# One late store of a cross-covariance attention kernel: transfers of 119 and 9 partitions in place of 92, 4, 32 and a half

## The chip, the cores and the metric

The kernel runs on one core of a Trainium2 chip. Its time is in device microseconds, the median of several runs; lower is better. The profile is of one execution, and its span runs from the core's first instruction to its last.

The core has a matrix engine (TensorE, here PE, with its weight loads as PEld), VectorE (DVE), ScalarE (ACT), GpSimd (POOL) and SyncE (SP). SP computes nothing here: it issues nearly all of the transfers between device memory and on-chip memory. The transfers themselves are carried out by sixteen DMA engines, which work through what has been issued.

## The reference

Q, K and V have 8 batches, 12 heads, 512 rows and 64 columns, in float32. For each of the 96 batch-heads, Q and K are normalised along the rows, their product over the rows gives a 64 x 64 matrix, its rows go through a softmax, and V is multiplied with the result:

```python
Q_norm = Q / (np.linalg.norm(Q, axis=-2, keepdims=True) + 1e-10)
K_norm = K / (np.linalg.norm(K, axis=-2, keepdims=True) + 1e-10)
attn = np.einsum('bhnd,bhne->bhde', Q_norm, K_norm)
attn = np.exp(attn - np.max(attn, axis=-1, keepdims=True))
attn = attn / (np.sum(attn, axis=-1, keepdims=True) + 1e-10)
return np.einsum('bhnd,bhde->bhne', V, attn).astype(np.float32)
```

The three inputs are read once (37.75 MB) and the output is written once (12.58 MB).

## The kernel before

**Tiling.** Four heads make a unit, of which there are 24, and two units make a step `s`, of which there are 12 (`S`). Q and K of a unit are loaded with 4 KB or 8 KB per partition, cast to bf16 by DVE (`cast_qk`, L208), and PE forms the Gram matrices of Q and K together (`grams`, L220), from which both the norms and the product come. DVE, ACT and POOL take them through the scaling and the softmax. V of two steps is loaded together (`load_v`, L189), cast, transposed on PE (`vtrans`, L294), and multiplied with the softmax result (`outs`, L309). The product is copied into a tile `so` by `ocopy` (L320, ACT or DVE).

**Stores.** A step has two output tiles, `so[s, 0]` and `so[s, 1]`, each of 128 partitions with two rows of 512 float32: the middle index `r` picks one row of 2 KB, and both are 512 KB together. `store(s, i)` (L198) writes tile `i` of step `s`. There are 24 stores; I write them (s, i). Each is one transfer of 128 partitions with both rows, L206, apart from one: `FEW = (S - 3, 1)` (L122), which is store (9,1). Four stores come behind it: (10,0), (10,1), (11,0) and (11,1), which is the last transfer of the kernel. A row of 2 KB on one partition is one DMA packet.

**Order.** The class `Order` (L22) plans the whole program ahead of time from estimated costs. Every piece of work has the engines it may run on, what it needs, what it stands behind, and a rank, and the plan picks the piece that can begin first, ranks deciding among those that are close. The program is then written in that order, so each engine's stream is fixed when the kernel is built. For the plan a store is one piece, of fixed cost `X`, however many transfers `store` makes of it.

**Issue on SP.** SP works its list off in order. A store waits for its two copies. It also waits for a completion semaphore: the transfers from SP and ACT take eight of them in turn, so a transfer can be issued only when the one eight places earlier has landed in full, that is when every DMA engine that had a share of it has reported. A DMA engine adds one to the semaphore when its share has landed. At the end of the program SP waits for the transfers still on their way (L493), and then the engines meet in a few barriers.

**Instructions.** PE has 4320 matmuls and weight loads. Instructions are also brought in through the DMA engines, which the profile shows as queues of their own: q8 with packets of 16 KB, q14 with packets of 8 KB.

Of the kernel before, what the change touches and what calls it, by code (L numbers as in the profile page):

```python
# [102 lines left out]
def kernel(  # L103
# [7 lines left out]
    nc = tc.nc  # L111
# [50 lines left out]
    qk32, v32, vb, qkb, gram, scr, kq, n2, r8, kqs, rq, lg, ex, ab, vps, vt, po, so = ({} for _ in range(18))  # L162
# [35 lines left out]
    def store(s, i):  # L198
        o = Of[s // 2, s % 2, i].rearrange("p r (j d) -> p r j d", d=D)
        if (s, i) == FEW:  # L200

            for a, b in ((0, 92), (92, 96), (96, 128)):
                nc.sync.dma_start(out=o[a:b, 0], in_=so[s, i][a:b, 0])
            nc.sync.dma_start(out=o[:, 1], in_=so[s, i][:, 1])
            return
        nc.sync.dma_start(out=o, in_=so[s, i])  # L206

# [139 lines left out]
    for i in range(NB["ab"]):  # L347
        a = const.tile([128, HU, 2 * D], BF16, name=f"ab{i}")
# [42 lines left out]
    for u in range(U):  # L391
        s, r = divmod(u, 2)
# [48 lines left out]
    for s in range(S):  # L441
        for x in range(4):
            i, k = divmod(x, 2)
            n = 4 * s + x - 2
            wait = [("oc", n // 4, n % 4)] if n >= 0 else []
            order = [("ou", s, x - 1) if x else back("ou", s, 1, 3)]
            piece(("ou", s, x), {"PE": 0.5}, [("vc", s // 2, *t) for t in turns(s // 2) if t[0] // 2 == k] + [("nm", s)] + wait, order, R["ou"] + 0.01 * s, outs, s, x)
            n = 2 * s + i - NB["so"]
            free = [("st", n // 2, n % 2)] if k == 0 and n >= 0 else []
            order = [("oc", s, x - 1) if x else back("oc", s, 1, 3)]  # L450
            piece(("oc", s, x), {"ACT": 0.6, "DVE": (0.68, BIAS["oc"])} if s >= BOTH else {"ACT": 0.6}, [("ou", s, x)] + free, order, R["oc"] + 0.01 * s, ocopy, s, x)
        for i in range(2):
            order = [("st", s, 0) if i else back("st", s, 1, 1)]
            piece(("st", s, i), {"DMA": X}, [("oc", s, 2 * i), ("oc", s, 2 * i + 1)], order, v_at(2 * s + i) + ST_LAG, store, s, i)
# [43 lines left out]
```

## Time and profile before

| what | value |
|---|---|
| median of 3 runs | 129.41 us (129.15 to 129.7) |
| span of the profiled execution | 127.43 us; the profile gives no other time for it |
| DMA traffic | 50.66 MB, 14958 packets, 398 GB/s in the mean |
| share of 16 DMA engines, kernel's transfers (q1 and q10) | 98.0% |
| PE busy | 77.0 us (60%) |
| DVE busy | 92.9 us (73%) |
| ACT busy | 72.3 us (57%) |
| POOL busy | 37.0 us (29%) |
| last copy into an output tile ends | 116.6 us |
| first transfer of store (9,1) issued | 111.44 us |
| store (11,1) issued | 120.75 us |

How to read the profile: the span is cut into 40 equal slices, and each digit is the busy share of an engine in a slice in tenths, 9 being 90% or more. The DMA row is the mean over the sixteen DMA engines, and the GB/s row what they moved. The queue table gives packets, megabytes and the share of the sixteen engines' time for each queue. A view can be limited to a window of the span, and then the 40 slices divide the window. The table of waits gives who waited for whom: microseconds in total, times, and the longest. Beside these the trace holds the time of every landing, one for each DMA engine's share of a transfer, and the start, length, size and queue of every DMA packet, but not the number of the DMA engine that moved it.

### The profile page before, as it was taken

To read this page: it belongs to the slowest core of one execution; us is meant where nothing else is said; L and a number is where in the kernel's file an instruction comes from. 1 tells how busy PE (TensorE), PEld (TensorE's weight loads), DVE (VectorE), ACT (ScalarE), POOL (GpSimd) and SP (SyncE) were. 2 spreads that over 40 slices of the span, in tenths; PEclk is the share of its full clock that TensorE was granted. 3 is DMA by queue.
4 is the path that set the end of the run, shared out by engine and by line. 5 is a ranking of instruction groups with operands and counts; after the bars stand their busy time and mean duration, and the time that the engine had idled before them with its cause. 6 is when DMAs were issued, how large, how long until landed. Compare 5 with 4: busy or idle time off the path is not lost.

```text
span 127.4 us, 4949 instructions
## 1 busy us (share of the span) xinstructions
PE 77.0 (60%) x2160; PEld 62.7 (49%) x2160; DVE 92.9 (73%) x142; ACT 72.3 (57%) x220; POOL 37.0 (29%) x39
## 2 busy tenths in 40 slices
PE   0065393994837679859475986777597729753000
PEld 0054372783636568647354674666386517541000
DVE  3344749949899899999974989998999499950000
ACT  4000441559877077886691897583848919996000
POOL 4006307300916903033077011303733160300000
PEclk9999999999985555999996799869959995999755
DMA  4999999999999999999999999999999999999991
GB/s 113 413 438 408 428 411 418 417 433 408 435 418 414 411 417 424 402 415 427 423 414 414 415 428 417 415 424 425 401 420 419 401 402 410 395 408 408 375 377 60
DMA packets 14958, 50.66 MB, mean 398 GB/s; under 512 B 1112, under 2 KB 1112, under 8 KB 13400
## 3 DMA queue, kind: packets, MB, share of 16 engines
q1 hardware_dynamic: 14648, 49.29, 95.9%
q10 hardware_dynamic: 288, 1.05, 2.1%
q8 instruction: 17, 0.28, 0.8%
q14 instruction: 5, 0.04, 0.1%
HBM read 37.75 MB, written 12.58 MB: 395 GB/s over the span
## 4 chain that ended last, share of the span: by engine, by line
DVE 36%; PE 21%; DMA 19%; issue 8%; ACT 5%; SPq 1%; DVEq 0%; ACTq 0%
DVE qkb L212 15%; DMA qk<-in_K_dram 14%; PE gram L232 12%; DVE scr L239 7%; DMA qk<-in_Q_dram 5%; DVE vt L168 4%; PE vps L301 4%; DVE ab L290 4%; PE po L318 3%; ACT so L166 3%; DVE n L251 2%; ACT ex L281 2%; DVE vb L168 2%; PE lg L275 1%; SPq L185 1%
## 5 line engine op out<-in xcount | busy, mean ns | idle before, releaser
L232 PE MATMUL gram<-qkb 32*128 32x128 bf16 x1536 | 36.7, 259 | 24.8 <-issue 8.5
L232 PEld LDWEIGHTS <-qkb 32*128 32x128 bf16 x1536 | 30.8, 116 | 29.7 <-issue 11.1
L212 DVE CAST qkb<-qk 128x1024 bf16<-128x1024 f32 x48 | 37.7, 810 | 9.6 <-DMA qk<-in_Q_dram 8.0
L170 POOL TENSOR_SCALAR vb<-v 128x1024 bf16<-128x1024 f32 x18 | 21.7, 1215 | 43.9 <-DMA v<-in_V_dram 39.0
L166 ACT COPY vt<-vps 128x1024 bf16<-128x1024 bf16 (+1 forms) x18 | 17.8, 986 | 18.8 <-PE vps L301 18.7
L166 ACT COPY so<-po 128x512 f32<-128x512 f32 x45 | 24.9, 593 | 6.1 <-PE po L318 5.8
L318 PE MATMUL po<-ab,vt 128*64 128x128 bf16 x384 | 19.1, 237 | 6.2 <-issue 2.6
L262 POOL TENSOR_TENSOR kqs<-kq,r 64x512 f32<-64x512 f32 x12 | 14.0, 1169 | 29.1 <-ACT r L258 16.2
L301 PE MATMUL vps<-identb,vb 128*128 128x128 bf16 x192 | 18.5, 253 | 4.8 <-POOL vb L170 3.5
L239 DVE SCALAR_TENSOR_TENSOR scr<-gram,eye 64x512 f32<-64x512 f32 x24 | 16.5, 687 | 4.9 <-PE gram L232 4.7
L318 PEld LDWEIGHTS <-vt 128*64 128x64 bf16 x384 | 13.4, 117 | 10.4 <-issue 5.7
L301 PEld LDWEIGHTS <-vb 128*128 128x128 bf16 x192 | 14.0, 113 | 7.9 <-POOL vb L170 4.2
L281 ACT ACTIVATE ex<-lg,rq 128x64 f32<-128x64 f32 x48 | 14.5, 322 | 2.7 <-PE lg L275 2.6
L166 ACT COPY kq<-gram 64x512 f32<-64x512 f32 x12 | 7.0, 582 | 13.2 <-DVE scr L239 12.9
L290 DVE TENSOR_TENSOR ab<-ex,rinv 64x256 bf16<-64x256 f32 x24 | 12.8, 534 | 0.6
L281 ACT ACTIVATION_READ_ACCUMULATOR ex<-lg,rq 128x1 f32 x48 | 10.2, 213 | 0.0
L168 DVE CAST vb<-v 128x1024 bf16<-128x1024 f32 x6 | 7.4, 1241 | 1.8 <-DMA v<-in_V_dram 1.7
L275 PE MATMUL lg<-eye,kqs 64*128 64x64 f32 x48 | 6.4, 259 | 3.2 <-issue 1.6
L251 DVE TENSOR_REDUCE n<-scr 128x8 f32<-128x512 f32 x12 | 8.1, 679 | 0.1
L168 DVE COPY vt<-vps 128x1024 bf16<-128x1024 bf16 (+1 forms) x8 | 8.0, 1022 | 0.2
L275 PEld LDWEIGHTS lg<-eye,kqs 64*128 64x128 f32 x48 | 4.5, 156 | 5.0 <-issue 2.5
L287 DVE RECIPROCAL rinv<-esum 128x4 f32<-128x4 f32 x12 | 2.0, 170 | 2.5 <-ACT ex L281 2.4
(17 smaller groups left out, 16.0 us busy)
## 6 DMA issues: line engine op xcount, KB each, us to landing
v<-in_V_dram SPq DMA_DIRECT2D x12, 1024.0 KB, 17.4
out_dram<-so SPq DMA_DIRECT2D x23, 512.0 KB, 11.2
qk<-in_Q_dram SPq DMA_DIRECT2D x8, 1024.0 KB, 16.8
qk<-in_K_dram SPq DMA_DIRECT2D x8, 1024.0 KB, 18.8
qk<-in_Q_dram SPq DMA_DIRECT2D x8, 512.0 KB, 11.9
qk<-in_K_dram SPq DMA_DIRECT2D x6, 512.0 KB, 12.6
qk<-in_K_dram ACTq DMA_DIRECT2D x2, 512.0 KB, 7.3
out_dram<-so SPq DMA_DIRECT2D x1, 256.0 KB, 7.2
```

The lines of the kernel that those rows point to most:

```text
L166: nc.scalar.copy(o, i)
L168: nc.vector.tensor_copy(o, i)
L170: nc.gpsimd.tensor_scalar(out=o, in0=i, scalar1=1.0, scalar2=0.0, op0=ALU.mult, op1=ALU.add)
L212: nc.vector.tensor_copy(qkb[u][:, :, x * D:(x + 1) * D], qk32[s][:, x, r])
L232: nc.tensor.matmul(gram[s][:, h, r, 0], x, x, start=(t == 0), stop=(t == (T if u < WIDE else J) - 1))
L239: nc.vector.scalar_tensor_tensor(out=scr[s][half], in0=gram[s][half, :, :, 0, half].rearrange("p h r d -> p (h r) d"), scalar=1e-20, in1=e ...
L262: (nc.vector if eng == "DVE" else nc.gpsimd).tensor_tensor(out=kqs[s][HI], in0=kq[s][HI], in1=r8[s][HI, :, None].to_broadcast([D, 2 * HU, ...
L275: nc.tensor.transpose(l[:, h, :], kqs[s][HI, 2 * h:2 * h + 2].rearrange("p r d -> p (r d)"), eye2[HI])
L281: nc.scalar.activation(e[:, h, :], lg[s][:, h, :], AF.Exp, scale=rq[s][:, h:h + 1], accum_out=z[:, h:h + 1])
L290: nc.vector.tensor_tensor(out=a[half, :, half], in0=e[half], in1=ri[half, :, None].to_broadcast([D, HU, D]), op=ALU.mult,)
L301: nc.tensor.transpose(ps[:, c, n, :], vb[w][:, J * c + j].rearrange("p r d -> p (r d)"), identb)
L318: nc.tensor.matmul(po[s, x][e * D:(e + 1) * D, j].rearrange("p r d -> p (r d)"), v, ab[s][:, h, :])
```

## The change

Store (9,1) is split differently. Before, row 0 of the tile leaves in three transfers, of partitions 0 to 91, 92 to 95 and 96 to 127, and row 1 in one transfer of all 128 partitions. After, both rows leave together, in one transfer of partitions 0 to 118 and one of partitions 119 to 127. SP issues two transfers fewer. The bytes are the same, the plan is the same, and all other stores and loads are as they were.

```diff
         o = Of[s // 2, s % 2, i].rearrange("p r (j d) -> p r j d", d=D)
         if (s, i) == FEW:
 
-            for a, b in ((0, 92), (92, 96), (96, 128)):
-                nc.sync.dma_start(out=o[a:b, 0], in_=so[s, i][a:b, 0])
-            nc.sync.dma_start(out=o[:, 1], in_=so[s, i][:, 1])
+            for a, b in ((0, 119), (119, 128)):
+                nc.sync.dma_start(out=o[a:b], in_=so[s, i][a:b])
             return
         nc.sync.dma_start(out=o, in_=so[s, i])
```

## The prediction

> **What bounds the kernel now.** I read the slices of the span first. DMA is at nine tenths or more in every slice between the first and the last, while no compute engine stays busy, so bytes on the sixteen DMA engines set the time. The queue table adds that almost all of it is the kernel's own traffic (q1), with 17 packets of instructions (q8) beside it.
>
> ```profile
> DMA  4999999999999999999999999999999999999991
> DMA packets 14958, 50.66 MB, mean 398 GB/s; under 512 B 1112, under 2 KB 1112, under 8 KB 13400
> q1 hardware_dynamic: 14648, 49.29, 95.9%
> q8 instruction: 17, 0.28, 0.8%
> ```
>
> So what a change in a late store can move is how the sixteen engines finish against each other. The window from 124.7 us to the end, in 40 slices of 0.07 us, shows it:
>
> ```profile
> DMA  3513110000000000000000000000000000000000
> GB/s 117 205 59 117 59 59 29 29 29 29 0 29 29 29 29 29 29 29 0 29 29 0 0 0 0 0 0 0 0 0 0 0 0 0 0 0 0 0 0 0
> ```
>
> 29 GB/s is one 2 KB packet per slice: from 125.1 to 126.2 us a single engine works and fifteen have finished. The same in the window from 125.5 us, where 9 packets are left:
>
> ```profile
> DMA packets 9, 0.02 MB, mean 9 GB/s; under 512 B 1, under 2 KB 1, under 8 KB 9
> ```
>
> Why one engine is last is in the trace's record of landings, sixteen per store (one per engine). In us:
>
> ```
> store (9,0):  116.39 116.46 116.54 116.86 116.87 117.23 117.63 118.48
>               119.16 119.17 119.27 119.28 119.29 119.39 119.42 120.69
> store (11,1): 123.55 123.57 123.68 124.34 124.37 124.75 125.11 125.12
>               125.13 125.21 125.22 125.24 125.34 125.36 125.50 126.53
> ```
>
> Ahead of the changed store, (9,1), there are seven early engines, one at 118.48, seven within 0.26 us, and one late. The 17 instruction packets (16 KB each) explain the groups: they last 967, 967, 948, 879, 881, 935, 929, 931 ns, then 960, 964, 951, 881, 879, 935, 931, 921, then 960. The same eight durations come round again, so eight engines take turns; each time an engine falls about 1.4 us back ((119.3-116.46)/2). Seven of the eight have had two; the seventeenth, at 117.65 us, gave one its third. That engine is the last at 126.53, and 0.9 us of barriers follow to the end of the span. Stores of 32 KB per engine keep this order, since each engine takes 1.27 us for one.
>
> **Profile against times.** The span is 127.43 us, the median of the runs 129.41 (129.15 to 129.7). The page gives no other time for the profiled execution, so I take 1.98 us outside the span as fixed. 0.5% of the time, 0.65 us, is about what a measurement of this kernel tells from no change.
>
> **The change, part by part.** How a transfer is spread is read from two rows. There are 71 issues; 71 x 16 is 1136 completions, the page counts 1112 small packets, 24 fewer. The parts of 92 and of 4 partitions complete on 4 engines each, which is 2 x 12. So 92 goes to 4, 4 to 4, 32 and 128 to 16: the largest number up to 16 that divides the partitions. By this 119 goes to 7 engines (17 partitions each) and 9 to 9. The Trainium skill ("DMA: Bandwidth & Descriptors", Why a DMA increments its semaphore by 16) has this rule, and adds that the lowest-numbered engines are used; it also tells of direct copies of the other descriptor path that put 8 partitions on an engine regardless, which is the third rival below.
>
> Packets of 2 KB per engine for store (9,1): before, the first four get 23+1+2+8 = 34, the other twelve 2+8 = 10. After, the first seven 17 x 2 = 34 and 2 more from the second transfer, 36; engines eight and nine get 2; the last seven get 0. Both sum to 256.
>
> Price of a packet: the late engine goes from 120.69 to 121.47 in store (9,1), 0.78 us for 10 packets and two completions; 32 KB stores take 1.27/16 = 0.080 us. The four engines of the 92 part landed it at 118.31, 118.70, 119.08, 119.47: 1.83 to 1.85 us after four of the early landings (116.46, 116.87, 117.23, 117.63), 23 packets at 0.080. So packing many onto few engines cost no more per packet there. The other end is a stretch of nine packets in a row between 98.5 and 99.7 us on one engine, 98 to 182 ns each, 0.13 in the mean: 34 packets would take 1.7 us longer. I take 0.080, the nearest row in place and kind, and keep 0.13 for the range.
>
> - Late engine: it loses 10 packets (if among the last seven) or 8 (if eighth or ninth). 126.53 - 0.78 = 125.75, or 126.53 - 0.61 = 125.92.
> - First four: two packets more, two completions fewer: 125.50 + 0.16 - 0.02 = 125.64 for the latest.
> - Fifth to seventh: if they are the remaining early ones (116.39, 116.54, 116.86), the latest gets 116.86 + 36 x 0.080 + 0.02 = 119.75, then four stores as the late engine did them (126.53 - 121.47 = 5.06): 124.81.
> - The engine at 118.48 with two packets: 118.48 + 0.17 + 5.06 = 123.7. The pack: 119.42 + 5.06 = 124.5.
>
> The end is 125.75 to 125.92. It can't go below 125.64 without the first four, so the gain is at most 0.89.
>
> Issues and waits. SP issues two transfers fewer (0.32 to 0.37 us each). Eight completion semaphores are used in turn, so the four stores behind wait for landings two places earlier: (11,0) and (11,1) for 115.55 and 116.85 in place of 119.65 and 120.69. They leave at about 115.6 and 116.9, not 119.72 and 120.75; (10,0) and (10,1) then wait for their copies, at about 113.1 and 114.6. Worth nothing at the end: only the three earliest engines ran dry (they did (10,1) by 120.25 and (11,0) at 122.28 to 122.40), and after the change they have work till 119.75. No other queue issues anything here, and the other engines' programs are untouched.
>
> ```profile
> SPq L493 <- DMA out_dram<-so: 5.3, 4, 1.6
> SPq L206 <- DMA out_dram<-so: 4.7, 4, 2.4
> SPq L204 <- DMA out_dram<-so: 0.9, 1, 0.9
> SPq L203 <- DMA out_dram<-so: 0.9, 1, 0.9
> ```
>
> These are SP's waits from 112 us on; I expect L206's to nearly vanish and those at the end (L493) to grow.
>
> Sum: gain 0.61 to 0.78, middle 0.70; 129.41 - 0.70 = 128.7. Own range of this case with the spread of the runs: 128.4 to 129.0.
>
> One rule of the skill bears on the late engine. The row: an instruction packet takes 879 to 967 ns and the engine under it lands 1.4 us late. "Runtime: NRT & Kernel Launch", Instruction fetch mechanics, says PE refills 256 instructions, 16 KB, at a time (4320 PE instructions make 17: agreed) and that the cost is "mostly hidden". By that the sixteen would be level and this change only a loss, the fifth to seventh ending 26 x 0.080 = 2.1 us behind the rest; the measured lag decides against it, and it gets no chance of its own.
>
> **Rivals.**
>
> *The seven take in an engine that is not early (slower).* The trace doesn't number engines. It shows that the four of the 92 part are early; that the next three are too is inferred from eight engines that fetch and eight that don't, and a block of eight. If one of the pack is among them: 119.42 + 2.90 + 5.06 = 127.38, 0.85 later, 130.3; with the late engine itself, 131.5. It decides from a landing of store (9,0) later than 126.53 - 5.06 - 2.90 = 118.57.
>
> *They take in the engine at 118.48.* 118.48 + 2.90 + 5.06 = 126.44: 0.09 gained, 129.3, no change. It is one of the eight that never fetch, so it may as well be fifth to seventh as eighth.
>
> *The split does nothing: 119 goes out eight partitions to an engine.* Then every engine gets 16, the late one 6 more: +0.48, 129.9. Against: 92 went to four engines. This stays inside 0.5%.
>
> *Few engines are slow.* At 0.13 us a packet the latest of the first four gets 125.64 + 1.7 = 127.3, 0.8 later, 130.2. Against: the 92 part's 0.080.
>
> **How the numbers follow.** Main case 0.62; an engine that is not early 0.20; the one at 118.48 0.10; no split 0.03; slow packets 0.05. In the main case 0.61 and 0.78 lie on both sides of 0.65; the late engine is first in the turn of eight, which may be the block's first (8 packets) or another (10), so I put somewhat over half of it, 0.38, above 0.5% and 0.24 within. Same is 0.24 + 0.10 + 0.03 = 0.37, slower 0.20 + 0.05 = 0.25. The range holds the main case with the spread, 118.48 and one of the pack: 128.4 to 130.3.
>
> **What would show it.** Right: the first transfer completes on 7 engines, small packets 69 x 16 - 9 - 7 = 1088; the one-engine stretch at the end shorter, the last landing near 125.8; SP's last four issues by 117 us. Wrong: several engines, about three, alone at the end and the last landing after 126.5 (first rival), or 1097 small packets, 7 missing and not 16 (no split). Should the late engine in other executions have had only two fetches, 125.50 against 125.64 would be left and nothing gained.

## The result and the profile after

The changed kernel takes 130.22 us (median of 7, 130.01 to 131.33) against 129.41 us (median of 7, 129.05 to 129.7): a ratio of 1.0079, with a 95% interval of 1.0054 to 1.0104. It is slower, by 0.8 us. I had forecast 128.7. The value lies in my range only because I had stretched the range up to 130.3 for my first rival; the sign, too, is that rival's.

The split itself went as forecast. The line of DMA packets and two of the queue lines, on the page of the changed kernel:

```profile
DMA packets 14934, 50.66 MB, mean 394 GB/s; under 512 B 1088, under 2 KB 1088, under 8 KB 13376
q1 hardware_dynamic: 14624, 49.29, 95.2%
q8 instruction: 17, 0.28, 0.8%
```

1088 small packets are 69 x 16 - 9 - 7: the part of 119 completes on 7 engines and the part of 9 on 9. The Trainium skill's rule ("DMA: Bandwidth & Descriptors", Why a DMA increments its semaphore by 16) and this trace agree. The 17 instruction packets are still there.

SP's waits for landings from 112 us on, who waited for whom, microseconds in total, times, longest (the lines of the program stand one lower than before):

```profile
SPq L492 <- DMA out_dram<-so: 9.1, 2, 7.9
SPq L205 <- DMA out_dram<-so: 1.9, 3, 0.8
```

The stores behind (9,1) wait 1.9 us for earlier landings in place of 4.7, where I had expected this wait nearly to vanish. They leave at 113.40, 114.82, 115.95 and 117.23 us, 0.2 to 0.4 us later than forecast. As forecast, leaving early earns nothing: the wait moved to the end of the program (L492, 9.1 us in place of 5.3).

Where the time went is in the last microseconds. The window from 124.7 to 128.5 us in 40 slices of 0.095 us, where one packet in a slice is 22 GB/s:

```profile
DMA  4333233322221121111111110000000000000000
GB/s 172 129 151 151 108 151 129 129 108 86 86 86 65 65 86 43 65 43 43 43 65 65 43 43 22 0 0 0 0 0 0 0 0 0 0 0 0 0 0 0
```

Before, one engine worked alone for 1.1 us. Now the work thins out over 2 us, with several engines for a while and two (43 GB/s) at the end. From 126.5 us on 15 packets are left. Two of them are completions, so two engines were still at work:

```profile
DMA packets 15, 0.03 MB, mean 13 GB/s; under 512 B 2, under 2 KB 2, under 8 KB 15
```

The landings of the changed kernel, one for each engine, say which two (us):

```
store (9,0):  116.58 116.65 116.69 116.95 117.09 117.39 117.91 118.60
              119.35 119.44 119.53 119.57 119.64 119.71 119.77 120.92
part of 119:  119.41 119.67 120.14 120.63 121.26 122.09 122.16
store (11,1): 121.88 121.95 122.24 124.67 124.70 124.72 124.76 124.85
              124.89 124.98 125.43 125.92 125.95 126.49 127.36 127.45
```

34 packets at 0.080 are 2.72 us. Taken off the seven landings of the 119 part, that leaves 116.69, 116.95, 117.42, 117.91, 118.54, 119.37, 119.44. These are seven places in the row of store (9,0): four early engines, the one at 118.60, and two of the pack (119.35 and 119.44). The two engines of the pack that took 36 packets are the two that end at 127.36 and 127.45. The engine at 118.60 is the third from the end, 126.49. The late engine, at 120.92, took none and was done at 125.9, near the 125.75 that I had reckoned for it. Three early engines had no share of the 119 part and ended at 121.88 to 122.24.

### The profile page after: what moved, and what is told of

The parts are those of the page before. It is cut to its first block, busy times and chain, and to the rows that moved or that the text cites. A ratio compares the mean times of both kernels' runs of the same rounds, so it can differ in the third digit from the quotient of the medians.

```text
span 128.5 us, 4947 instructions
## 1 busy us (share of the span) xinstructions
PE 80.0 (62%) x2160; PEld 65.3 (51%) x2160; DVE 93.1 (72%) x142; ACT 72.4 (56%) x220; POOL 37.0 (29%) x39
## 2 busy tenths in 40 slices
DMA packets 14934, 50.66 MB, mean 394 GB/s; under 512 B 1088, under 2 KB 1088, under 8 KB 13376
## 4 chain that ended last, share of the span: by engine, by line
DVE 38%; DMA 21%; PE 19%; issue 6%; ACT 6%; DVEq 0%; SPq 0%; ACTq 0%
DMA qk<-in_Q_dram 21%; DVE qkb L211 15%; PE gram L231 11%; DVE scr L238 7%; DVE ab L289 6%; PE vps L300 4%; DVE vb L168 3%; DVE vt L168 2%; PE po L317 2%; DVE n L250 2%; ACT ex L280 2%; ACT so L166 2%; ACT vt L166 2%; DVE so L168 1%; PE lg L274 1%
## 5 line engine op out<-in xcount | busy, mean ns | idle before, releaser
L231 PE MATMUL gram<-qkb 32*128 32x128 bf16 x1536 | 37.3, 264 | 24.7 <-DVE qkb L211 9.0
L231 PEld LDWEIGHTS <-qkb 32*128 32x128 bf16 x1536 | 31.7, 119 | 29.1 <-DVE qkb L211 10.9
L211 DVE CAST qkb<-qk 128x1024 bf16<-128x1024 f32 x48 | 35.7, 771 | 9.1 <-DMA qk<-in_Q_dram 7.5
L317 PE MATMUL po<-ab,vt 128*64 128x128 bf16 x384 | 20.4, 249 | 5.5 <-DVE ab L289 2.2
L300 PE MATMUL vps<-identb,vb 128*128 128x128 bf16 x192 | 19.5, 260 | 3.3 <-POOL vb L170 2.0
L317 PEld LDWEIGHTS <-vt 128*64 128x64 bf16 x384 | 14.4, 125 | 10.1 <-issue 4.7
L289 DVE TENSOR_TENSOR ab<-ex,rinv 64x256 bf16<-64x256 f32 x24 | 14.4, 599 | 0.6
L168 DVE CAST vb<-v 128x1024 bf16<-128x1024 f32 x6 | 8.0, 1333 | 1.7 <-DMA v<-in_V_dram 1.7
L274 PE MATMUL lg<-eye,kqs 64*128 64x64 f32 x48 | 6.9, 274 | 3.1 <-issue 1.6
```

What stands on the lines that cost most here:

```text
L168: nc.vector.tensor_copy(o, i)
L211: nc.vector.tensor_copy(qkb[u][:, :, x * D:(x + 1) * D], qk32[s][:, x, r])
L231: nc.tensor.matmul(gram[s][:, h, r, 0], x, x, start=(t == 0), stop=(t == (T if u < WIDE else J) - 1))
L274: nc.tensor.transpose(l[:, h, :], kqs[s][HI, 2 * h:2 * h + 2].rearrange("p r d -> p (r d)"), eye2[HI])
L289: nc.vector.tensor_tensor(out=a[half, :, half], in0=e[half], in1=ri[half, :, None].to_broadcast([D, HU, D]), op=ALU.mult,)
L300: nc.tensor.transpose(ps[:, c, n, :], vb[w][:, J * c + j].rearrange("p r d -> p (r d)"), identb)
```

## The experiments

**Theory 1** is the first rival: two of the seven engines fetch PE's instructions, were not early, and end last with 36 packets. **Theory 2** was left from the prediction's own reasoning: all seven were early, and the shape of the split (packets crowded on few engines, or four stores issued earlier) costs by itself. The edits are to the kernel before, unless another is named.

### Which engines are early

The record of packets has no engine numbers, but a transfer of n partitions, n up to 16, should land on n engines. If these are always the first n, transfers of growing n number the engines one after the other. In store (9,1):

```diff
-            for a, b in ((0, 92), (92, 96), (96, 128)):
-                nc.sync.dma_start(out=o[a:b, 0], in_=so[s, i][a:b, 0])
-            nc.sync.dma_start(out=o[:, 1], in_=so[s, i][:, 1])
+            a = 0
+            for n in (4, 5, 6, 7, 8, 9, 10, 11, 12, 13, 14, 15, 14):
+                nc.sync.dma_start(out=o[a:a + n], in_=so[s, i][a:a + n])
+                a += n
```

> Store (9,1) leaves as thirteen transfers of 4, 5, 6, ... 15 and 14 partitions, both rows. A transfer of n partitions should land on the first n engines (two packets each), so each adds one engine to those of the one before, and its landings tell whether the n-th engine is an early one. Theory 1 (two of the fifth to seventh engines fetch PE's instructions and were not early): the parts of 5, 6 and 7 add one engine about 1.0 us and two about 1.5 to 2.5 us behind the latest of the first four, and the parts of 8 and 9 add two of the earliest. Theory 2 (the seven were all early, and the packets became slow or the earlier issue of the four stores behind hurt): the parts of 5, 6 and 7 add engines that land with the first four, and late ones come only from the eighth or ninth on. The time itself means little here: thirteen small transfers use up the eight semaphores; some 130 to 132 us.

It took 132.52 us (one run). The landings of store (9,0) and of the first parts:

```
store (9,0): 116.35 116.43 116.64 116.88 116.90 117.20 117.81 118.60
             119.10 119.14 119.25 119.27 119.38 119.38 119.61 120.76
part of 4:   116.83 117.06 117.39 118.00
part of 5:   117.02 117.23 117.57 118.17 118.80
part of 6:   117.21 117.41 117.77 118.34 119.00 119.47
part of 7:   117.38 117.58 117.94 118.52 119.18 119.31 119.67
part of 8:   117.17 117.56 117.75 118.12 118.69 119.36 119.50 119.87
```

Each part moves an engine's landing by some 0.18 us, so the new one in each row stands out. The fifth engine comes in at 118.80 (0.2 after 118.60), the sixth at 119.47, the seventh at 119.31: the last two are of the pack. The eighth comes in at 117.17, before all others, and the ninth with it in the part of 9. That is theory 1's order. The distances are smaller than I had put them: I had the fifth 1.0 us and the sixth and seventh 1.5 to 2.5 us behind the latest of the first four in the same part, and they are 0.6, 1.1 and 0.8 behind, since the first four had taken earlier parts. With each one's own 0.18 taken off, the sixth and seventh stand 1.5 and 1.3 us behind the fourth's landing of store (9,0), 117.81. From the part of 10 on the parts were issued too late to tell.

The same with parts from 10 up, for the other engines:

```diff
-            for n in (4, 5, 6, 7, 8, 9, 10, 11, 12, 13, 14, 15, 14):
+            for n in (10, 11, 12, 13, 14, 15, 48, 5):
```

> Store (9,1) leaves as transfers of 10, 11, 12, 13, 14, 15, 48 and 5 partitions, both rows, to number the engines from the tenth on: each of the first six parts should land on one engine more than the one before it. The first map showed the first four early, the fifth 0.8 us behind them, the sixth and seventh at the place of the engines that have had two instruction packets, the eighth and ninth early. If eight engines fetch, six of the seven from the tenth to the sixteenth must be fetching ones: one early, five with two packets, and the one with its third. Theory 1 (taking turns in the order of numbers from the first fetching engine): the late one is the lowest fetching engine, which is the sixth, and then its landings in the first map would have been 1.4 us later than they were; so the turn starts at the tenth or eleventh. Theory 2 (order of turns not by number): the late one may be any of seven. The time itself means little: some 130 to 132 us.

130.68 us (one run). The part of 10 landed at 116.61, 116.67, 116.98, 117.21, 117.64, 118.20, 118.67 and then three times in the pack's place (119.35, 119.44, 119.51): the sixth, the seventh and the tenth. The parts of 11, 12, 14 and 15 each added one more of the pack, at 119.33, 119.51, 119.46 and 119.63, and the part of 13 added one at 120.95, the late engine. One early engine (116.89 in store (9,0)) came in nowhere: it is the sixteenth. So the engines that fetch for PE are the sixth, the seventh and the tenth to the fifteenth, and the late one in this execution was the thirteenth. My expectation that the turn starts at the lowest numbers fell.

### What the split is worth

No split at all, store (9,1) like the others:

```diff
-            for a, b in ((0, 92), (92, 96), (96, 128)):
-                nc.sync.dma_start(out=o[a:b, 0], in_=so[s, i][a:b, 0])
-            nc.sync.dma_start(out=o[:, 1], in_=so[s, i][:, 1])
+            nc.sync.dma_start(out=o, in_=so[s, i])
```

> Store (9,1) as one transfer of 128 partitions like all others, 16 packets to each engine. Theory 1 (an engine ends at its own lateness ahead of the store plus 0.080 us a packet): the late engine gets 6 packets more than before, 126.53 + 0.48 = 127.01, 129.9 us; every other engine ends by 125.9. So the changed kernel, at 130.2, should be 0.3 slower than no split at all. Theory 2 (concentrated packets or earlier issue cost by themselves): no concentration here, but three transfers fewer ahead of the last four stores; if the earlier issue was what hurt, at least as slow as the changed kernel, 130.2 or more.

129.92 us (ratio to the kernel before 1.0043, 1.0024 to 1.0063), as theory 1 had it. The last landings were 127.08 for the late engine and 125.88 for the next. The window from 124.7 to 127.5 us shows that engine alone for over a microsecond (one packet in a slice of 0.07 us is 29 GB/s):

```profile
GB/s 205 205 146 205 205 234 176 205 146 88 88 29 29 29 29 29 29 29 0 29 29 29 29 29 29 29 0 29 29 0 0 0 0 0 0 0 0 0 0 0
```

The last four stores leave early here too (113.40 to 116.81 us), and it is 0.3 faster than the changed kernel, which speaks against a cost of the early issue.

Half of the change, 119 and 9 partitions for row 0 alone:

```diff
-            for a, b in ((0, 92), (92, 96), (96, 128)):
+            for a, b in ((0, 119), (119, 128)):
                 nc.sync.dma_start(out=o[a:b, 0], in_=so[s, i][a:b, 0])
```

> 119 and 9 partitions for row 0 alone, row 1 as one transfer of 128 as before. The first seven engines get 17 + 1 + 8 = 26 packets, two get 9, seven get 8. Theory 1: the two fetching engines among the seven end at 119.42 + 26 x 0.080 + 0.03 + 5.06 = 126.59, the late engine at 126.53 - 0.16 = 126.37; end 126.6, 129.45 us (129.3 to 129.6), the same as before. Theory 2 (a loss by the shape itself, so half of it for half the change, with one transfer fewer to issue in place of two): 129.8.

129.53 us (ratio 1.0022, 0.9997 to 1.0046; 12 runs): theory 1's 129.45, not theory 2's 129.8. The two engines of the pack and the late one end together, at 126.18, 126.30 and 126.38. The same window:

```profile
GB/s 146 88 88 117 88 88 88 59 88 88 59 88 59 88 88 59 59 29 0 0 0 0 0 0 0 0 0 0 0 0 0 0 0 0 0 0 0 0 0 0
```

Two or three engines (59 to 88) work to within a slice of the end, where the kernel before had one. But three of the twelve runs took 130.42 to 130.75 us, which I come back to.

### The instruction packet that makes the late engine

The seventeenth packet of 16 KB is to go, by giving PE fewer instructions. The edit leaves work out: the Gram matrices of the last unit are summed over half of the rows, so the output of four heads is not the one asked for. Both kernels had it:

```diff
-        for t in range(T if u < WIDE else J):
+        n = J if u == U - 1 else T
+        for t in range(n):
...
-                nc.tensor.matmul(gram[s][:, h, r, 0], x, x, start=(t == 0), stop=(t == (T if u < WIDE else J) - 1))
+                nc.tensor.matmul(gram[s][:, h, r, 0], x, x, start=(t == 0), stop=(t == n - 1))
```

> The kernel before, with the Gram matrices of the last unit summed over 8 of their 16 steps, so 64 PE instructions fewer (4256 in place of 4320; the last four heads are computed from half of the rows). This is to take away the seventeenth instruction packet, and with it the late engine. If the packet makes the lateness: 16 packets on q8, the late engine joins the pack, and the latest of the first four sets the end at 125.50 in place of 126.53: 128.4 us. If the lateness has another cause: 129.4.

> The changed kernel with the same 64 PE instructions fewer (the last four heads computed from half of the rows). Theory 1 (the sixth and seventh engines, with two instruction packets each and 36 packets of the store, set the end): the seventeenth packet lies on another engine, so the end stays near 127.4 and the time at 130.2. Rival (the late engine still has a part in the end): the time falls by up to 1.0, to 129.2.

The kernel before fell to 128.41 us (ratio 0.9923, 0.991 to 0.9937), the changed one stayed at 130.11 (ratio 1.0058 to the kernel before, 1.0044 to 1.0073). The queue lines and the end window (124.7 to 127.5 us) of the shortened kernel before:

```profile
q8 instruction: 16, 0.26, 0.7%
...
GB/s 205 234 88 146 117 59 29 29 0 29 29 0 0 0 0 0 0 0 0 0 0 0 0 0 0 0 0 0 0 0 0 0 0 0 0 0 0 0 0 0
```

With 16 packets nothing works alone for a microsecond any more; the last landing is 125.81 us, of one of the first four engines. In the shortened changed kernel the last two landings are 127.06 and 127.18, so there the late engine had no part in the end. Its queue line and the same window, with two engines (59) nearly to the end:

```profile
q8 instruction: 16, 0.26, 0.7%
...
GB/s 88 146 146 88 117 117 117 88 59 117 117 59 88 88 88 59 59 88 59 29 59 59 59 29 59 59 59 29 29 29 0 0 0 0 0 0 0 0 0 0
```

The seventeenth packet is what sets the end of the kernel before, and the sixth and seventh engines are what set it after the change.

### A split by the map, and one that failed in part

If the late engine is always the thirteenth, transfers that use at most twelve engines leave it out:

```diff
-            for a, b in ((0, 92), (92, 96), (96, 128)):
-                nc.sync.dma_start(out=o[a:b, 0], in_=so[s, i][a:b, 0])
-            nc.sync.dma_start(out=o[:, 1], in_=so[s, i][:, 1])
+            for r, a, b in ((0, 0, 36), (0, 36, 128), (1, 0, 108), (1, 108, 128)):
+                nc.sync.dma_start(out=o[a:b, r], in_=so[s, i][a:b, r])
```

> Store (9,1) split by the map: row 0 in transfers of 36 and 92 partitions (12 and 4 engines), row 1 in 108 and 20 (12 and 10 engines). Packets: first four 37, fifth to tenth 14, eleventh and twelfth 12, thirteenth (the late one) to sixteenth none. Theory 1: the late engine ends at 120.69 + 5.06 = 125.75, the latest of the first four at 117.63 + 37 x 0.080 + 0.04 + 5.06 = 125.69, the sixth and seventh at 119.42 + 14 x 0.080 + 0.03 + 5.06 = 125.63; end 125.75, 128.6 us (128.4 to 128.9). Theory 2 (uneven splits cost by themselves): at or above the kernel before, 129.4.

129.46 us, no better than the kernel before (ratio 0.9996, 0.9977 to 1.0014). But the twelve runs form two groups: three at 128.65 to 128.68, which is the forecast, and nine at 129.37 to 129.75. The profile is of one of the three; its end window (124.7 to 127.5 us) has no engine alone for long:

```profile
DMA  6665533121100000000000000000000000000000
GB/s 263 263 234 205 205 146 117 59 88 59 59 29 0 0 0 0 0 0 0 0 0 0 0 0 0 0 0 0 0 0 0 0 0 0 0 0 0 0 0 0
```

The lengths of the instruction packets point to the reason. In ns, in order, from the profiles of four kernels:

```
before:       967 967 948 879 881 935 929 931 | 960 964 951 881 879 935 931 921 | 960
even split:   954 882 881 934 991 924 962 960 | 947 879 879 941 938 924 960 967 | 948
119, row 0:   934 931 922 965 1022 948 879 882 | 934 931 925 962 960 947 879 886 | 935
before, short: 879 941 933 931 1014 961 954 881 | 879 942 938 922 967 962 954 879
```

It is the same round of eight, entered at another place; the two near 880 mark it (a packet at about 41 us, the fifth, is longer than its place would give in three of the four). If the execution of the kernel before begins with the first of the round, the even split's begins with the third, that with row 0 alone with the sixth, the shortened kernel's with the fifth. So the engine that gets the seventeenth packet is not the same in all of these profiles. (Those of the change, of no split and of both maps begin with the first, as that of before does, and the second map's late engine was the thirteenth.) The profiles are of different kernels; that the engine also differs between executions of one kernel is inferred from the two groups of times. With the even split the thirteenth to fifteenth engines have no packets of store (9,1) and the other five that fetch have 12 or 14; a late engine among those would end 12 to 14 x 0.080 = 1.0 to 1.1 us later than 125.75, which would be 129.6 to 129.8 us, a little more than measured. Three engines of eight against three runs of twelve fit. In the same way the three runs of row 0 alone at 130.42 to 130.75 fit a late sixth or seventh engine (120.69 + 26 x 0.080 + 0.03 + 5.06 = 127.86, 130.7 us), and the one run of the changed kernel at 131.33 fits my rival's 131.5 for it. That the runs of each group had these engines late was not seen, since one execution of each was profiled; that profiles begin at different places of the round was.

### Without the seventeenth packet

If the late engine changes, a split that spares one engine helps only where that one is late. So I took the packet away without leaving work out. The kernel has a second layout for a last unit, with 64 partitions to a head and half of the matmuls:

```diff
-    WIDE = U
+    WIDE = U - 1
```

> The kernel before with WIDE = U - 1: the last unit's Q and K are laid out with 64 partitions to a head, and its Gram matrices take 32 matmuls in place of 64, with nothing left out. PE has 4256 instructions, as in the shortened kernels. If the seventeenth instruction packet is what sets the end of the kernel before: it is gone, the latest of the first four ends at about 125.5 to 125.8, and the two loads of 2 KB packets cost 16 x 2 x 0.080 - 8 x 2 x 0.155 = 0.08 more: 128.5 us (128.2 to 128.7). If it was the left-out work that made the shortened kernel faster: 129.4.

And with it fewer packets for the first four engines:

```diff
-            for a, b in ((0, 92), (92, 96), (96, 128)):
+            for a, b in ((0, 76), (76, 80), (80, 128)):
```

> The same, and row 0 of store (9,1) in parts of 76, 4 and 48 partitions: the first four engines get 19 + 1 + 3 + 8 = 31 packets, the other twelve 11. In the shortened kernel before, the end was the latest of the first four at 125.81, the pack ending at 125.51. Moving three packets from each of the four and one to each of the twelve: 125.81 - 0.24 = 125.57 and 125.51 + 0.08 = 125.59, so 0.2 faster than the kernel above: 128.3 us. If the split of this store no longer matters once no engine is late: the same as the kernel above.

128.51 us (ratio 0.994, 0.9925 to 0.9954) and 128.34 us (ratio 0.9928, 0.9913 to 0.9943). Their runs spread over 0.2 us, 128.46 to 128.63 (six runs) and 128.28 to 128.48 (five), with no second group. The second beats both kernels, the changed one by 1.9 us. The 0.17 between them is in the last landings, 125.83 for one engine in the first, 0.3 us after all others, and 125.59 in the second, where nine engines land between 125.31 and 125.59. The second's queue line and end window (124.7 to 127.5 us):

```profile
q8 instruction: 16, 0.26, 0.7%
...
GB/s 263 205 234 176 146 117 88 0 0 0 0 0 0 0 0 0 0 0 0 0 0 0 0 0 0 0 0 0 0 0 0 0 0 0 0 0 0 0 0 0
```

There are still three packets (88 GB/s) in the last slice with any: no engine works alone.

## Why the prediction was wrong

**What held.** That sixteen DMA engines end against each other, and that the last of them sets the time. The forecasts of the experiments add packets at 0.080 us to an engine's landing, or move its end as the profile of before gave it. Six of seven came out: 129.9, 129.45, 128.4, 130.2, 128.5 and 128.3 were forecast, and 129.92, 129.53, 128.41, 130.11, 128.51 and 128.34 measured. The seventh, the even split, had 128.6 forecast and 129.46 measured. Held too: 119 goes to 7 engines and 9 to 9; 34 packets in a row cost 0.080 each (2.72 us), not the 0.13 of the range's other end; the late engine is made by the seventeenth instruction packet, was relieved as reckoned, and ended at 125.9; the waits of SP moved to the end, and the last landing comes out of the packets without them (below).

**What failed** is one step: "Fifth to seventh: if they are the remaining early ones (116.39, 116.54, 116.86)", which gave 124.81. They were the engine at 118.48 and two of the pack, so that the conditions of the first and the second rival both held. So the seven did not end at 125.64 at most; two of them ended at 119.44 + 36 x 0.080 + 0.02 + 5.06 = 127.40 (127.36 and 127.45 measured). The engine at 118.48 alone would have made no change, as that rival says: 126.44 by its sum, 126.49 measured. The early engines that I had counted on are the eighth, the ninth and the sixteenth.

The step rested on "eight engines that fetch and eight that don't, and a block of eight". The first half was read from the trace, the second was not: the trace of before numbers four engines, and nothing in it says that the next three are like them. With four early engines placed and twelve left, of which three were early, the chance that the fifth to seventh are exactly those three is small if one knows nothing more. I gave the main case 0.62 because a block is the tidy arrangement, and the first rival 0.20; on what the trace showed, the rival's share should have been the larger. Its price was right: 130.3 for 130.22. The 131.5 for the late engine among the seven stands beside the one run at 131.33, but that this run had it so was not seen.

A smaller error of the same kind: the experiment with the even split took the late engine to be the same in every execution. In the median of the two kernels compared it changes little, since before the change all engines that fetch have 10 packets. The even split missed its forecast in nine runs of twelve, and a late engine that changes fits these times.

Two readings in the prediction are off without bearing on the sign. The 1.98 us outside the span is too large: in the profiled executions of the other ten kernels the time is 1.78 to 1.90 us more than the span, so the execution profiled before was probably 0.1 to 0.2 us faster than the median. And 4320 instructions making 17 packets of 256 is no confirmation of that division: 4256 would make 17 by it as well (16.6), and the kernels with 4256 had 16.

The Trainium skill ("Runtime: NRT & Kernel Launch", Instruction fetch mechanics) calls the cost of crossing into a new block "mostly hidden". In the time of this kernel it isn't: one packet of 16 KB fewer was worth 0.8 to 1.0 us (129.41 to 128.41, 129.3 to 128.51).

## What to carry to other kernels

Where the DMA engines are full to the end, compare the landings engine by engine, not their mean: the time is that of the last engine, and what other queues fetch is part of its load. Before moving load to "the idle engines", find out which engines they are, by small transfers of growing partition counts; a likely arrangement is no reading. And where the load that makes one engine late seems to move about between executions, take that load away: a split that spares one engine helps only the executions in which that engine is the late one.

## What the runs showed of the hardware

- The engines that fetch PE's instructions are the sixth, the seventh and the tenth to the fifteenth of the sixteen, by the two maps: these eight land last. Each packet of 16 KB (0.88 to 1.02 us) puts its engine about 1.4 us behind, as the landings before the change have it ((119.3 - 116.46)/2, and 120.69 against 119.3). Why the fifth engine, which fetches none, lands 0.85 us after the other early ones (118.48 against 117.63) stays open.
- By the lengths of the packets they take turns in a fixed round of eight. Profiles began with the first, third, fifth and sixth place of it, the place in the profile of before being called the first. What decides the place was not found.
- A transfer of n partitions used n engines for every n from 4 to 15 (each part of the maps completed on as many); 119 used 7, 108 and 36 used 12, 20 used 10, 92 and 76 used 4.
- Whether the numbers of the fetching engines are the same on every chip was not tried beyond the two maps, which ran on two chips. The profiles of before, of the change and of both maps show the same four groups in the landings of store (9,0).
